# Routing of the last token tile in an attention, convolution and expert layer on one core: o-projection halves adjoined, weight splits moved to other places

## The chip, the cores and the metric

One core of a Trainium2 chip runs the whole layer in one launch. The metric is device time in microseconds, the median of several executions.

## What is computed

The kernel computes one layer for 1024 prompt tokens and 64 sample tokens (1088 rows of 1024 features). An attention branch and a gated short convolution are merged by sigmoid gates into m, and then come the parts that this document is about, all in float32 (shortened from the reference):

```
x = x + m @ w_o
h2 = rmsnorm(x, g_ffn)
g_logit = h2 @ w_rg + b_rg                  # 4 groups, the best one is taken
e_logit = (h2 @ w_re + b_re)[group]         # 8 experts in it, the best two are taken
gate = softmax(g_logit)[group] * top2(softmax(e_logit)) / sum(top2)
for each of 32 experts e, over the rows that chose it:
    y = (silu(h2 @ w1[e]) * (h2 @ w3[e])) @ w2[e]
x = x + sum over the two chosen experts of gate * y
x = x + sigmoid(rmsnorm(x, g_ple) @ w_pg) * (p @ w_ple)
```

The layer also returns the attention latents, the rotary keys and the convolution state.

## The kernel before, in words

The 1088 rows are nine tiles: tiles 0 to 7 of 128 rows and tile 8 of 64. A float32 product is made from three products of a rounded number type: each operand is split into a rounded part (`hi`, L56, a cast on ACT) and the rest (`lo`, L59, a subtraction, on VectorE unless another engine is named), and `mm3` (L61) multiplies hi by hi, hi by lo and lo by hi.

**The o-projection and the router.** `o_mm(i, b, fill)` makes half b (512 columns) of m @ w_o for tile i: 8 steps of k with three matmuls each. `fill` names functions to be called behind step k, which is how the steps of one tile's routing are put between another tile's matmuls on TensorE. `o_add` (L1051) adds a half to x on VectorE. `o_sq` squares a row on ACT and makes 1/rms on POOL (`rstd`, L84 and L85). `o_h2` (L1065) makes h2 on VectorE and stores h2 (`h2d`, L1067) and x (`x1d`, L1068) to DRAM from SP's queue. `o_tr` transposes four blocks of x (L1076) and splits them, `o_rt` multiplies them by the router's weights (L1087, L1089) and copies the result (lgT, L1093), `o_lg` transposes it back (L1098) and scales it into the logits lg (L1099, VectorE).

**Routing.** `route1(i)` is 20 short VectorE operations on the logits of tile i (L1123 to L1152): the group, the two experts, the one-hot matrices, and the running counts mc. `route2` makes each row's rank within its expert (L1158, L1159 on TensorE, L1161 to L1165 on VectorE; the two `am` operations are L1165). `route3` adds the tile to `tab` (L1172), the table of which row sits in which place of which expert. The tiles are routed in the order 0 to 5, 8, 6, 7. After the last tile the table becomes integer row numbers, `idx` (L1272).

**Experts.** `gather` (L1281) fetches up to 96 rows of h2d that an expert got, by an indirect DMA issued from POOL, into one of three buffers xg that were set to zero (L1341). `x_tr` transposes and splits the gathered rows (L1291, tiles xTh and xTl). Six weight blocks per expert, 128x1024 each, are loaded by SP into `eraw` (`e_load`, L894) and split by `e_hi` into weh on ACT and by `e_lo` into wel. SP takes its work in order, and a weight load also waits until the load five places ahead of it has landed (`w_dma`, DEEP = 5). There are 30 places for eraw, five experts' worth. The places of expert 3 are those of weights of the o-projection's first halves, and so come free when the last first half is done. `gate_values` (L1365 to L1376) turns logits into the gates, and `overflow_counts` (L1380 to L1409) counts rows beyond 96 per expert.

**What sets the order.** From the first `o_mm` up to `order.close()` the order on all five engines is that in which the code issues the work, written by hand. Behind `order.close()` a scheduler sets it. The code around the change:

```
    o_mm(7, 0, {5: [(route2, 5)]})
    o_add(7, 0)
    o_mm(8, 0, {0: [(route3, 5)]})
    ...
    e_load(4, (1, 4))
    o_tr(7, 1)
    o_h2(7)
    e_hi(0, 0)
    e_lo(0, 0, nc.gpsimd)
```

Of the kernel before, what the change touches and what calls it, by code (L numbers as in the profile page):

```python
# [7 lines left out]
F32 = mybir.dt.float32  # L8
# [3 lines left out]
AF = mybir.ActivationFunctionType  # L12
OP = mybir.AluOpType
# [7 lines left out]
D = 1024  # L21
# [4 lines left out]
EPS = 1e-6  # L26
# [8 lines left out]
A2 = 2 * T  # L35
DEEP = 5


@with_exitstack
def body(ctx, tc, a):  # L40
# [69 lines left out]
    def bank():  # L110
        return pb.tile([128, 512], F32, name="bk", tag="bk")
# [896 lines left out]
    gffn = xp2.tile([128, D], F32, name="gffn")  # L1008
    x1_, rs_, h2_, hb6, prt = {}, {}, {}, {}, {}

# [42 lines left out]
    def o_sq(i):  # L1053
        h2 = xp2.tile([128, D], F32, name="h2", bufs=1)
        ss = xp2.tile([128, 1], F32, name="ss4", bufs=2)
        n = TN[i]
        nc.scalar.activation(h2[:n], x1_[i][:n], AF.Square, accum_out=ss[:n])
        rs_[i] = xp2.tile([128, 1], F32, name="rs4", bufs=2)
        rstd(rs_[i][:n], ss[:n], 1.0 / D, 1)
        h2_[i] = h2  # L1060

    def o_h2(i):
# [46 lines left out]
    def small(name, *sh, dt=F32, bufs=2):  # L1109
        return xp2.tile([128] + list(sh), dt, name=name, bufs=bufs)  # L1110

    def g4(x):
        return x[:, :, None].to_broadcast([128, 4, 8])

    ed = edesc[:, None, :].to_broadcast([128, 4, 8])

    def route1(i):
        gl = lg[:, i, 0:4]
        el = lg[:, i, 4:36].rearrange("p (g e) -> p g e", g=4)
        d1, d2, oh1, oh2, es2 = (small(n, 4, 8, bufs=1) for n in ("d1", "d2", "oh1", "oh2", "es2"))  # L1120
        wg, wm = small("wg", 4), small("wm", 1)
        wm1, wm2 = small("wm1", 4), small("wm2", 4)
        V_.tensor_reduce(out=m1[:, i], in_=el, axis=AX.X, op=OP.max)  # L1123
        V_.tensor_reduce(out=gm[:, i:i + 1], in_=gl, axis=AX.X, op=OP.max)
# [7 lines left out]
        V_.scalar_tensor_tensor(out=es2, in0=oh1, scalar=-1e30, in1=el, op0=OP.mult, op1=OP.add)  # L1132
        V_.tensor_tensor(out=M[:, 0, i].rearrange("p (g e) -> p g e", g=4), in0=oh1, in1=g4(goh[:, i]), op=OP.mult)
        V_.tensor_reduce(out=m2[:, i], in_=es2, axis=AX.X, op=OP.max)
        V_.tensor_tensor(out=d2, in0=es2, in1=g4(m2[:, i]), op=OP.is_ge)
# [15 lines left out]
        else:  # L1151
            V_.tensor_tensor(out=mc, in0=MCs[r], in1=ms, op=OP.add)  # L1152
        MCs[r + 1] = mc

    def route2(i):
# [22 lines left out]
    for i in range(6):  # L1178
# [13 lines left out]
        if i >= 1:  # L1192
# [8 lines left out]
    e_load(1, (2, 5))  # L1201
    o_mm(7, 0, {5: [(route2, 5)]})
    o_add(7, 0)
    o_mm(8, 0, {0: [(route3, 5)]})
    o_add(8, 0)
    e_load(3)
    o_mm(8, 1, {6: [(o_tr, 8, 0)]})
    o_add(8, 1)
    o_sq(8)
    o_mm(6, 1, {1: [(o_tr, 8, 1), (o_h2, 8)], 3: [(o_rt, 8, 0, 8)],  # L1210
                5: [(o_lg, 8), (route1, 8)], 6: [(o_tr, 6, 0)]})
    o_add(6, 1)
    o_sq(6)
    e_load(4, (2, 5, 0, 3))
    o_mm(7, 1, {1: [(o_tr, 6, 1), (o_h2, 6)], 2: [(route2, 8)], 3: [(o_rt, 6, 0, 8)], 4: [(route3, 8)], 
                5: [(o_lg, 6), (route1, 6)], 6: [(o_tr, 7, 0)]})
    o_add(7, 1)
    o_sq(7)
    wbs.close()
# [37 lines left out]
    e_load(4, (1, 4))  # L1257
    o_tr(7, 1)
    o_h2(7)
    e_hi(0, 0)  # L1260
    e_lo(0, 0, nc.gpsimd)
    o_rt(7, 0, 8)
    route2(6)
    o_lg(7)
    route3(6)
    route1(7)
    for j in range(1, 6):
        e_hi(0, j)
    e_lo(0, 1, nc.gpsimd)
    route2(7)  # L1270
# [69 lines left out]
    for e in range(3):  # L1340
        nc.gpsimd.memset(xgs[e], 0.0)  # L1341
        gather(xgs[e][:CAP], idx[:CAP, 0, e:e + 1])
    for j in range(2, 6):
        e_lo(0, j)
    e_load(5)
    order.close()


    eps_, ep = opened("moe", bufs=2)
    x_tr(0, xgs[0], 0, ep, CAP)  # L1350
    x_tr(0, xgs[0], 1, ep, CAP)
    scr, pos = ep.tile([128, D], F32, name="y", bufs=NY), [0]
# [57 lines left out]

    gate_values()
    overflow_counts()

# [370 lines left out]
```

## Time and profile before

| | us |
|---|---|
| median of 3 runs | 1350.8 |
| the runs | 1348.19, 1350.80, 1350.96 |
| the profiled execution | 1351.81 |
| its span in the profile | 1349.8 |
| TensorE matmul busy | 1268.6 (94% of the span) |
| VectorE busy | 848.0 (63%) |
| ACT busy | 649.7 (48%) |
| POOL busy | 323.8 (24%) |

The shares are averages over the span. The profile's row of forty slices shows one place in the last half where TensorE is busy less than half of the time: the slice after 877 us has the digit 4 for TensorE and 6 for the granted clock. The chain of work that ended last is almost only TensorE's work at the program's end.

### The profile page before, as it was taken

How to read it: one execution, taken by the hardware profiler on the slowest of the kernel's cores; microseconds unless marked ns; L12 is line 12 of the kernel's file. 1: busy time of each engine (PE TensorE's matmuls, PEld its weight loads, DVE VectorE, ACT ScalarE, POOL GpSimd, SP SyncE). 2: the span in 40 equal slices, each digit the busy share in tenths (PEclk: the TensorE clock that was granted, in tenths of full speed). 3: DMA queues.
4: the chain of work that ended last, by engine and by line, in shares of the span. 5: the costliest groups of instructions: out<-in, count | busy, mean ns of one | idle time of the engine just before them, and what ended most of it. 6: DMA issues, size and time to landing. Idle time of an engine off the chain costs nothing. (4 is left out here: it accounts for less than half of the span.)

```text
span 1349.8 us, 20413 instructions
## 1 busy us (share of the span) xinstructions
PE 1268.6 (94%) x7235; PEld 1100.1 (81%) x7235; DVE 848.0 (63%) x1627; ACT 649.7 (48%) x1276; POOL 323.8 (24%) x375
## 2 busy tenths in 40 slices
PE   7999999998998999999999999749999999999998
PEld 6999999998987988888998888537666666667886
DVE  6433243325675466666659755678988889884743
ACT  6212142223344455555545211338888888886322
POOL 2000001124663333333315200232222222210210
PEclk9999999999998999999999999869999999999999
DMA  5111298734477523242257656769999999967511
GB/s 197 64 34 45 78 355 299 276 117 137 138 188 223 176 69 125 86 150 73 82 197 265 247 201 225 252 185 350 364 346 346 340 345 347 346 235 272 204 39 55
DMA packets 106057, 272.36 MB, mean 202 GB/s; under 512 B 13521, under 2 KB 42689, under 8 KB 105922
## 3 DMA queue, kind: packets, MB, share of 16 engines
q1 hardware_dynamic: 89968, 220.29, 47.1%
q0 software_dynamic: 15840, 50.68, 11.7%
q8 instruction: 58, 0.95, 0.3%
q14 instruction: 45, 0.37, 0.1%
q10 hardware_dynamic: 146, 0.07, 0.0%
HBM read 211.14 MB, written 67.19 MB: 206 GB/s over the span
## 5 line engine op out<-in xcount | busy, mean ns | idle before, releaser
L59 DVE TENSOR_TENSOR wel<-eraw,weh 128x1024 fp32r<-128x1024 f32 x190 | 226.3, 1220 | 34.4 <-ACT weh L56 32.4
L56 ACT CAST weh<-eraw 128x1024 fp32r<-128x1024 f32 x192 | 196.0, 1054 | 11.7 <-PE bk L64 10.7
L769 POOL TENSOR_TENSOR P<-P,ri 128x128 f32<-128x128 f32 (+8 forms) x72 | 77.2, 1077 | 129.2 <-DVE ri L768 109.6
L63 PE MATMUL bk<-wel,xTh 128*96 128x512 f32 x256 | 103.5, 404 | 1.5 <-DVE wel L59 1.4
L62 PE MATMUL bk<-weh,xTh 128*96 128x512 f32 x256 | 102.5, 400 | 1.7 <-ACT xTh L56 1.7
L64 PE MATMUL bk<-weh,xTl 128*96 128x512 f32 x256 | 103.1, 403 | 0.0
L1337 POOL DMA_INDIRECT Yd<-y,idx x32 | 41.3, 1292 | 227.2 <-ACT y L1334 217.5
L59 DVE TENSOR_TENSOR wl<-w_r,wh 128x1024 fp32r<-128x1024 f32 x28 | 34.3, 1225 | 75.7 <-ACT wh L56 75.3
L62 PE MATMUL bk<-hTAh,wh 128*128 128x384 f32 x224 | 76.6, 342 | 1.8 <-ACT hTAh L56 1.8
L63 PE MATMUL bk<-hTAl,wh 128*128 128x384 f32 x224 | 76.4, 341 | 0.0
L64 PE MATMUL bk<-hTAh,wl 128*128 128x384 f32 x224 | 76.1, 340 | 0.0
L62 PE MATMUL fg<-hTBh,fw 128*128 128x384 f32 (+1 forms) x224 | 74.9, 334 | 0.3 <-ACT fgm L605 0.2
L56 ACT CAST wh<-w_r 128x1024 fp32r<-128x1024 f32 x28 | 29.4, 1050 | 91.8 <-PE bk L63 86.3
L64 PE MATMUL fg<-hTBh,fw 128*128 128x384 f32 (+1 forms) x224 | 73.3, 327 | 0.0
L63 PE MATMUL fg<-hTBl,fw 128*128 128x384 f32 (+1 forms) x224 | 73.1, 326 | 0.0
L62 PE MATMUL bk<-hTBh,wh 128*128 128x384 f32 (+1 forms) x192 | 62.2, 324 | 0.0
L63 PE MATMUL bk<-hTBl,wh 128*128 128x384 f32 (+1 forms) x192 | 62.0, 323 | 0.0
L64 PE MATMUL bk<-hTBh,wl 128*128 128x384 f32 (+1 forms) x192 | 61.8, 323 | 0.0
L63 PEld LDWEIGHTS bk<-wel,xTh 128*96 128x96 f32 x256 | 41.7, 163 | 22.2 <-DVE wel L59 7.8
L62 PE MATMUL bk<-weh,ath 128*96 128x512 f32 x128 | 50.9, 397 | 8.8 <-ACT ath L56 8.8
L755 DVE TENSOR_REDUCE nm<-S 128x1 f32<-128x128 f32 (+8 forms) x72 | 50.8, 706 | 12.7 <-PE S L64 11.6
L62 PEld LDWEIGHTS bk<-weh,xTh 128*96 128x96 f32 x256 | 41.6, 162 | 19.3 <-ACT xTh L56 3.3
(782 smaller groups left out, 3750.8 us busy)
## 6 DMA issues: line engine op xcount, KB each, us to landing
eraw<-in_we_dram SPq DMA_DIRECT2D x192, 512.0 KB
fw<-wsd POOLq DMA_DIRECT2D x32, 512.0 KB, 4.3
w_r<-in_wing_dram SPq DMA_DIRECT2D x28, 512.0 KB
gm_r<-gscr SPq DMA_DIRECT2D x16, 544.0 KB
wsd<-wh SPq DMA_DIRECT2D x16, 512.0 KB
wsd<-wl SPq DMA_DIRECT2D x16, 512.0 KB
xy<-Yd SPq DMA_DIRECT2D x16, 512.0 KB
vd<-V SPq DMA_DIRECT2D x10, 512.0 KB
```

The source lines that it names most:

```text
L56: nc.scalar.copy(dst, src)
L59: (eng or nc.vector).tensor_tensor(out=dst, in0=src, in1=h.bitcast(F32), op=OP.subtract)
L62: r = nc.tensor.matmul(ps, sh, mh, start=first, stop=False)
L63: nc.tensor.matmul(ps, sh, ml, start=False, stop=False)
L64: nc.tensor.matmul(ps, sl, mh, start=False, stop=last)
L755: nc.vector.tensor_reduce(out=nm, in_=s, axis=AX.XY, op=OP.max, negate=True)
L769: nc.gpsimd.tensor_tensor(out=P[:, :nk], in0=P[:, :nk], in1=ri.to_broadcast([128, nk]), op=OP.mult)
L1337: nc.gpsimd.indirect_dma_start(out=Yd[:, :], out_offset=bass.IndirectOffsetOnAxis(ap=col, axis=0), in_=buf, in_offset=None, bounds_check=A ...
```

## The change

The o-projection halves of tile 7 are made last and next to each other. Before, the halves stood in the order (6,0), (7,0), (8,0), (8,1), (6,1), (7,1); now it is (6,0), (8,0), (8,1), (6,1), (7,0), (7,1). The steps of tile 6's routing, which stood behind (6,1) and partly behind (7,1), are put between the matmuls of (7,0) and (7,1); `route1` is cut in two for this. Tile 7's square is made by halves (`o_sq_half`), and its first transposes and first router matmuls stand within (7,1). POOL makes no weight splits any more: the six `lo` splits of expert 0 are VectorE's, two behind the gate values and four behind the transposition of the first gathered rows. Six `hi` casts stand behind the router instead of around it. Ten matmuls whose result nobody reads stand behind the last tab matmul (WARM). The weight loads of expert 3 are issued later. All line numbers rise by 1, by 15 behind `o_sq`, and by more further on.

```diff
...
+    def o_sq_half(i, b):
+        n = TN[i]
+        if b == 0:
+            h2_[i] = xp2.tile([128, D], F32, name="h2", bufs=1)
+            sqh[i] = xp2.tile([128, 2], F32, name="ss4h", bufs=1)
+        c = slice(512 * b, 512 * b + 512)
+        nc.scalar.activation(h2_[i][:n, c], x1_[i][:n, c], AF.Square, scale=1.0 / 32, accum_out=sqh[i][:n, b:b + 1])
+        if b == 1:
+            ss = sqh.pop(i)
+            rs = rs_[i] = xp2.tile([128, 1], F32, name="rs4", bufs=2)
+            nc.gpsimd.tensor_scalar(out=rs[:n], in0=ss[:n, 0:1], scalar1=ss[:n, 1:2], scalar2=EPS, op0=OP.add,
+                                    op1=OP.add)
+            nc.gpsimd.tensor_tensor(out=rs[:n], in0=rs[:n], in1=mhalf[:n, :1], op=OP.pow)
...
-    def route1(i):
+    def route1a(i):
...
+    def route1b(i):
+        d2, oh2, es2, wm2 = r1.pop(i)
         V_.tensor_reduce(out=m2[:, i], in_=es2, axis=AX.X, op=OP.max)
...
-    o_mm(7, 0, {5: [(route2, 5)]})
-    o_add(7, 0)
-    o_mm(8, 0, {0: [(route3, 5)]})
+    o_mm(8, 0, {5: [(route2, 5)]})
     o_add(8, 0)
-    e_load(3)
-    o_mm(8, 1, {6: [(o_tr, 8, 0)]})
+    o_mm(8, 1, {0: [(route3, 5)], 6: [(o_tr, 8, 0)]})
     o_add(8, 1)
     o_sq(8)
-    o_mm(6, 1, {1: [(o_tr, 8, 1), (o_h2, 8)], 3: [(o_rt, 8, 0, 8)],
-                5: [(o_lg, 8), (route1, 8)], 6: [(o_tr, 6, 0)]})
+    e_load(4, (2,))
+    o_mm(6, 1, {1: [(o_tr, 8, 1), (o_h2, 8)], 3: [(o_rt, 8, 0, 8)], 4: [(o_lg, 8), (route1, 8)],
+                6: [(o_tr, 6, 0)]})
     o_add(6, 1)
     o_sq(6)
-    e_load(4, (2, 5, 0, 3))
-    o_mm(7, 1, {1: [(o_tr, 6, 1), (o_h2, 6)], 2: [(route2, 8)], 3: [(o_rt, 6, 0, 8)], 4: [(route3, 8)], 
-                5: [(o_lg, 6), (route1, 6)], 6: [(o_tr, 7, 0)]})
+    e_load(4, (0, 3))
+    o_mm(7, 0, {0: [(o_tr, 6, 1)], 1: [(route2, 8), (o_h2, 6)], 2: [(o_rt, 6, 0, 8)], 3: [(route3, 8)],
+                4: [(o_lg, 6), (route1a, 6)]})
+    o_add(7, 0)
+    e_load(3)
+    e_load(4, (5,))
+    route1b(6)
+    o_mm(7, 1, {3: [(route2, 6), (o_tr, 7, 0), (o_sq_half, 7, 0)], 5: [(route3, 6)], 7: [(o_rt, 7, 0, 4)]})
     o_add(7, 1)
-    o_sq(7)
+    o_sq_half(7, 1)
+    o_tr(7, 1)
+    o_h2(7)
+    o_rt(7, 4, 8)
+    o_lg(7)
...
     e_load(4, (1, 4))
-    o_tr(7, 1)
-    o_h2(7)
-    e_hi(0, 0)
-    e_lo(0, 0, nc.gpsimd)
-    o_rt(7, 0, 8)
-    route2(6)
-    o_lg(7)
-    route3(6)
     route1(7)
-    for j in range(1, 6):
+    for j in range(6):
         e_hi(0, j)
-    e_lo(0, 1, nc.gpsimd)
     route2(7)
     route3(7)
...
-    for j in range(2, 6):
-        e_lo(0, j)
-    e_load(5)
-    order.close()
+    for _ in range(WARM):
+        nc.tensor.matmul(bank(), wsl[0, 0][0][:, 0:128], wsl[0, 0][0][:, 0:512], start=True, stop=True)
...
-    x_tr(0, xgs[0], 0, ep, CAP)
-    x_tr(0, xgs[0], 1, ep, CAP)
...
     gate_values()
+    e_lo(0, 0)
+    e_lo(0, 1)
+    x_tr(0, xgs[0], 0, ep, CAP)
+    x_tr(0, xgs[0], 1, ep, CAP)
+    for j in range(2, 6):
+        e_lo(0, j)
+    e_load(5)
+    order.close()
     overflow_counts()
```

On POOL, from 1/rms of tile 7 (rs) to the first gather, the kernel before has (rs of tile 6 ends in its first row)

```order
L85 TENSOR_TENSOR rs_9389<-rs_9389,mhalf 128x1
L84 TENSOR_SCALAR rs_9513<-ss_9511 128x1
L85 TENSOR_TENSOR rs_9513<-rs_9513,mhalf 128x1
L59 TENSOR_TENSOR wel<-eraw,weh 128x1024 x2
L1341 MEMSET xg_9635 128x1024
L1281 DMA xg_9635<-h2d,idx 96x1024
```

and the changed kernel

```order
L86 TENSOR_TENSOR rs_9353<-rs_9353,mhalf 128x1
L1073 TENSOR_SCALAR rs_9534<-ss4h 128x1
L1075 TENSOR_TENSOR rs_9534<-rs_9534,mhalf 128x1
L1364 MEMSET xg_9634 128x1024
L1304 DMA xg_9634<-h2d,idx 96x1024
```

The two weight splits are gone from between 1/rms and the zeroing of xg.

On VectorE, from the rank (rnk, am) and idx of the last tile on, the kernel before has these rows; y and gates are the gate values and, from L1382 on, the overflow counts:

```order
L1162 TENSOR_REDUCE rnk<-pr 128x2
L1165 TENSOR_SCALAR am<-c_7557,rnk 128x96 x2
L1272 TENSOR_SCALAR idx<-tab 96x64
L59 TENSOR_TENSOR wel<-eraw,weh 128x1024 x4
L1365 TENSOR_TENSOR y<-lg,gm 128x36
L1372 TENSOR_REDUCE y<-m_7553 128x9
L1397 MEMSET y 1x24
L1368 TENSOR_REDUCE y<-y 128x9
L1374 SCALAR_TENSOR_TENSOR y<-y 128x9
L1375 RECIPROCAL gates<-y 128x9
L1376 TENSOR_TENSOR gates<-gates,y 128x9
L59 TENSOR_TENSOR xTl_9671<-bk,xTh_9670 128x384
```

In the changed kernel, from the end of the gate values on (idx stands six rows ahead of the first row shown):

```order
L1390 TENSOR_REDUCE y<-m_7553 128x9
L1392 SCALAR_TENSOR_TENSOR y<-y 128x9
L1393 RECIPROCAL gates<-y 128x9
L1394 TENSOR_TENSOR gates<-gates,y 128x9
L60 TENSOR_TENSOR wel<-eraw,weh 128x1024 x2
L1400 TENSOR_SCALAR y<-bk 128x32
L60 TENSOR_TENSOR xTl_9686<-bk,xTh_9685 128x384
L1402 CAST y<-y 128x32
L60 TENSOR_TENSOR xTl_9695<-bk,xTh_9694 128x384
L60 TENSOR_TENSOR wel<-eraw,weh 128x1024 x4
L1403 TENSOR_SCALAR y<-y 128x32
```

The four splits that followed idx at once now follow the gate values (two, in place of POOL's) and the two xTl of the first expert (four), and the overflow operations come later.

On SP, from the load of x for tile 8 to the last stores of h2 and x (tile 7), the kernel before issues

```order
L1013 DMA x_9179<-in_x_dram 64x1024
L894 DMA eraw<-in_we_dram 128x1024 x8
L1067 DMA h2d<-h_9281 64x1024
L1068 DMA x1d<-x_9179 64x1024
L894 DMA eraw<-in_we_dram 128x1024 x4
L1067 DMA h2d<-h_9386 128x1024
L1068 DMA x1d<-x_9029 128x1024
L894 DMA eraw<-in_we_dram 128x1024 x2
L1067 DMA h2d<-h_9510 128x1024
L1068 DMA x1d<-x_9031 128x1024
L894 DMA eraw<-in_we_dram 128x1024 x162
```

and the changed kernel

```order
L1014 DMA x_9179<-in_x_dram 64x1024
L895 DMA eraw<-in_we_dram 128x1024 x3
L1082 DMA h2d<-h_9243 64x1024
L1083 DMA x1d<-x_9179 64x1024
L895 DMA eraw<-in_we_dram 128x1024 x2
L1082 DMA h2d<-h_9350 128x1024
L1083 DMA x1d<-x_9029 128x1024
L895 DMA eraw<-in_we_dram 128x1024 x7
L1082 DMA h2d<-h_9506 128x1024
L1083 DMA x1d<-x_9031 128x1024
L895 DMA eraw<-in_we_dram 128x1024 x164
```

Seven weight loads stand ahead of the last h2d store, where there were two; the five are missing ahead of the store of tile 8 (the 64-row one).

## Rows read from the trace of the kernel before

**Rows 1.** Windows: length, busy us of PE, PEld, DVE, ACT, POOL, clock, DMA share, GB/s.

```profile
870.00:880.00 10.00, 4.59 (x27) 3.88 (x28) 8.14 (x16) 7.56 (x10) 7.04 (x5) 0.51 0.59 216
880.00:890.00 10.00, 0.73 (x3) 0.41 (x2) 8.87 (x32) 0.33 (x2) 5.06 (x2) 0.50 0.43 134
890.00:900.00 10.00, 3.41 (x14) 2.66 (x15) 1.92 (x8) 0.96 (x2) 4.44 (x5) 0.50 0.73 217
900.00:910.00 10.00, 9.69 (x47) 6.63 (x46) 9.60 (x19) 7.72 (x10) 0.96 (x1) 0.95 0.59 175
910.00:920.00 10.00, 10.00 (x51) 7.20 (x50) 9.64 (x14) 9.14 (x14) 2.47 (x2) 1.00 0.99 329
...
960.00:1100.00 140.00, 135.73 (x670) 95.46 (x669) 123.11 (x144) 116.93 (x174) 34.48 (x28) 1.00 0.99 346
```

**Rows 2.** Timeline of TensorE: start, length, line, operation, count, idle before and releaser.

```profile
859.60 0.65 PE L1076 MATMUL bk<-ident,x 128*128 128x128 f32 x4 [1.38 <-DVE x L1051]
...
864.98 0.31 PE L1098 MATMUL bk<-id,lgT 72*128 72x36 f32 x2
...
866.56 0.39 PE L63 MATMUL bk<-wo71l,mT 128*128 128x512 f32 x1
866.79 0.40 PE L64 MATMUL bk<-wo71h,mT 128*128 128x512 f32 x1
870.10 1.01 PE L1076 MATMUL bk<-ident,x 128*128 128x128 f32 x4 [2.91 <-DVE x L1051]
...
873.93 0.64 PE L1098 MATMUL bk<-id,lgT 72*128 72x36 f32 x2 [0.33 <-ACT lgT L1093]
...
896.59 1.51 PE L1291 MATMUL bk<-ident,xg 96*128 96x96 f32 x8 [12.79 <-DMA xg<-h2d,idx]
...
899.85 0.63 PE L63 MATMUL bk<-wel,xTh 128*96 128x512 f32 x1
```

**Rows 3.** Timeline of VectorE, 863 to 898 us.

```profile
863.59 0.45 DVE L1165 TENSOR_SCALAR am<-c,rnk 128x96 fp32r<-128x96 f32 x2
...
874.16 4.98 DVE L1165 TENSOR_SCALAR am<-c,rnk 128x96 fp32r<-128x96 f32 x2
878.17 0.97 DVE L1099 SCALAR_TENSOR_TENSOR lg<-bk,rs,brt 128x36 f32<-128x36 f32 x1
...
883.83 0.22 DVE L1272 TENSOR_SCALAR idx<-tab 96x64 int32<-96x64 f32 x1 [0.46 <-PE tab L1172]
883.97 4.62 DVE L59 TENSOR_TENSOR wel<-eraw,weh 128x1024 fp32r<-128x1024 f32 x4
...
898.01 0.56 DVE L59 TENSOR_TENSOR xTl<-bk,xTh 128x384 fp32r<-128x384 f32 x1 [8.03 <-ACT xTh L56]
```

**Rows 4.** Timeline of POOL, 872 to 968 us.

```profile
872.77 5.41 POOL L59 TENSOR_TENSOR wel<-eraw,weh 128x1024 fp32r<-128x1024 f32 x2 [0.59 <-ACT weh L56]
...
884.92 4.65 POOL L1281 DMA_INDIRECT xg<-h2d,idx  x1 [5.85 <-issue]
...
890.83 1.00 POOL L1281 DMA_INDIRECT xg<-h2d,idx  x1 [0.28 <-POOL xg L1341]
...
967.31 1.15 POOL L1281 DMA_INDIRECT xg<-h2d,idx  x1 [0.30 <-PE bk L1317]
```

**Rows 5.** Timeline of VectorE under the gather at 967.31.

```profile
966.39 3.50 DVE L59 TENSOR_TENSOR wel<-eraw,weh 128x1024 fp32r<-128x1024 f32 x3 [0.20 <-ACT weh L56]
```

**Rows 6.** DMA queues from 880 to 892 us: packets, MB, share of 16 engines.

```profile
q1 hardware_dynamic: 526, 1.92, 50.2%
```

**Rows 7.** Timeline of SP's DMA issues, 832 to 874 us.

```profile
832.59 0.43 SPq L1068 DMA_DIRECT2D x1d<-x  x1
836.24 0.49 SPq L1013 DMA_DIRECT2D x<-in_x_dram  x1
...
873.69 0.33 SPq L1067 DMA_DIRECT2D h2d<-h  x1
```

**Rows 8.** Page, costliest groups: busy, mean ns, idle before and its releaser.

```profile
L59 DVE TENSOR_TENSOR wel<-eraw,weh 128x1024 fp32r<-128x1024 f32 x190 | 226.3, 1220 | 34.4 <-ACT weh L56 32.4
```

More of the change, by code (lines that the diff above doesn't have):

```diff
@@ L36 @@
 DEEP = 5
+WARM = 10
 @with_exitstack
@@ L1008, in body @@
     gffn = xp2.tile([128, D], F32, name="gffn")
-    x1_, rs_, h2_, hb6, prt = {}, {}, {}, {}, {}
+    x1_, rs_, h2_, hb6, prt, sqh = {}, {}, {}, {}, {}, {}
     def o_load(i):
@@ L1115, in body @@
     ed = edesc[:, None, :].to_broadcast([128, 4, 8])
-    def route1(i):
+    r1 = {}
+    def route1a(i):
         gl = lg[:, i, 0:4]
@@ L1122, in route1 @@
         wm1, wm2 = small("wm1", 4), small("wm2", 4)
+        r1[i] = d2, oh2, es2, wm2
         V_.tensor_reduce(out=m1[:, i], in_=el, axis=AX.X, op=OP.max)
@@ L1153, in route1 @@
         MCs[r + 1] = mc
+    def route1(i):
+        route1a(i)
+        route1b(i)
     def route2(i):
```

## The prediction

> **What bounds the kernel now.** I read three views in turn. First the windows, for the engines by stretch [rows 1]. From 960 to 1100 us, in the loop over the experts, TensorE is busy 135.73 of 140 us and VectorE 123.11: the loop is TensorE's, VectorE is close behind, and the DMA share is 0.99. Only 3 per cent is free there, so time that the loop gets at its start or loses there is kept to the end. Between 870 and 900 it is different: TensorE is busy 4.59, 0.73 and 3.41 of 10 us, at a granted clock of 0.50 to 0.51, the lower of its two levels (1.2 of 2.4 GHz). That is the hole which the change works on: the routing of the last tile, then the first gather.
>
> Then TensorE's timeline through the hole [rows 2]. The last o-projection matmul starts at 866.79 and ends 0.40 later. The transposes of tile 7 begin at 870.10, after 2.91 us of waiting for VectorE's sum; the transposes of the first gathered rows begin at 896.59, after 12.79 us of waiting for the gather to land. So the hole is one chain: sum, transposes, router, logits, routing on VectorE, idx, gather, landing. Whatever shortens it moves the expert loop forward.
>
> Last, VectorE and POOL in that stretch [rows 3, 4]. The pair of am operations, 0.45 us for tile 8, takes 4.98 us at 874.16, while POOL runs its two lo splits from 872.77 to 878.18; the logits of tile 7 stand behind that pair and start at 878.17, though their matmuls ended at 873.93 + 0.64 = 874.57. idx ends at 883.83 + 0.22 = 884.05. POOL starts the first gather at 884.92 and is at it for 4.65 us; the second takes 1.00. It landed at 896.59, 7.02 after the 889.57 at which POOL was done.
>
> **Part one: idx comes earlier.** Terms, all on the chain:
> - The sum of tile 7 no longer stands behind tile 6's whole routing, which is now split and interleaved. TensorE has nothing to do for 2.91 us in the kernel before; what has to remain is about the 0.7 us of one half's addition and its hand-over. I take 2.2 off, and put 0.3 back, since routing steps of tile 5 now stand in front of shorter runs of matmuls and may wait: -1.9. Bounds: 0 (the sum is as late as before) to -2.3.
> - With so short a wait I expect the clock to stay up. A wait of 1.38 us at 859.60 left it up: these four transposes took 0.65, those of tile 7 after 2.91 us of waiting took 1.01, and the two logit matmuls 0.31 against 0.64 [rows 2]. That is 0.36 + 0.33, and 0.1 for the square done by halves: -0.8 (bounds 0 to -1.2, if the router's last matmuls halve as well).
> - With no split on POOL, the am pair of tile 6 takes its 0.45 and is done inside the last matmuls. The logits start behind their own matmul: they end some 0.3 after it, where they ended at 878.17 + 0.97 = 879.14, or 4.57 after it: -4.3. This is the surest term.
> - Two gate operations of 0.1 us each leave the routing of tile 7: -0.2.
>
> Sum: 7.2 us; idx ends near 876.8. The Trainium skill ("SBUF — State Buffer", section "Who interferes with whom") says that a tensor_scalar in its two-port form and GpSimd lock each other out for a whole instruction. The row of 4.98 us for the am pair agrees.
>
> **Part two: the first gather.** The change puts VectorE's four splits (4.62 us from 883.97) behind the gather's issue. Is it they that made it 4.65 us? For it: they ended at 888.59, and the gather at 889.57, which is 0.98 later, the length of an undisturbed gather [rows 3, 4]. Against it: the gather at 967.31 ran under three splits back to back (966.39, 3.50 us) and took 1.15 [rows 4, 5], as the others of the loop did. And it is the first gather of the program: something paid once would look the same. No instruction queue moved anything from 880 to 892, only q1 did [rows 6]; that speaks against code being fetched then, but not against other first-time work. I hold the once-paid cost for likelier: 4.65 stays, and with it the start 0.87 after idx. Bounds of this term: 0 to -(4.65 - 0.96) - (0.87 - 0.29) = -4.3, the second from POOL's usual 0.28 between two steps.
>
> Two rules of the Trainium skill pull the same way. "GPSIMD Engine Reference", section "Instruction dispatch", says that the first call of a freshly loaded kernel pays about 6 us once; by that page the gather would stay long and the sum would keep its 7.2. "SBUF — State Buffer" (same section as above) says that a tensor_tensor has no two-port form and takes only the read side of the shared ports, while making descriptors needs the write side; by that the splits never held the gather up, which speaks against what this change would gain there. The 1.15 us at 967.31 agrees with it; the 0.98 above does not.
>
> **Part three: what is given back.** Two splits that POOL made are now VectorE's, but lie in its wait for the landing (nothing else was there: its next work after the gate values began at 898.01). The four others now stand behind the transposed lo halves of the first expert, so behind the landing. There VectorE is busy 9.60 and 9.64 of 10 us [rows 1], so 4.62 us of extra work find 0.40 + 0.36 us free; the rest delays the splits of the second expert, and TensorE with them: +3.9. Bounds: 0 (the overflow operations, which move back behind splits, make room) to +4.62. I take 3.9 since both engines are nearly full there.
>
> **Part four: costs that I put at nothing.** Ten filler matmuls follow the last tab matmul: at most 0.63 each as at the low clock [rows 2], 6.3 us, in TensorE's own 12.79 us of waiting. Their cover goes only if the gather lands within 6.3 us of idx, and its transfer alone took 7.02. Would they keep the clock up? They end some 5 us or more before the landing, and 2.91 us without work were enough for 1.01 us transposes; so nothing is gained. If it were, the first expert's six matmuls of 0.63 would be shorter, by less than 1.5 us. Six ACT casts move behind the lgT copy: ACT is free there.
>
> On SP, seven weight loads are put ahead of the two stores of tile 7, where there were two. Their buffers are free when the first half of tile 7 is done, one half (24 matmuls at 0.23) before the last matmul's end: 867.2 - 5.6 = 861.6. At the loop's 346 GB/s [rows 1] a 512 KB load takes 1.5 us, seven 10.6: the last lands near 872.2, about when h2 of tile 7 is ready. A store took 3.65 us, from 832.59 to the load at 836.24 that waited for it [rows 7]. So h2d lands near 875.9, a little ahead of idx at 876.8, and the gather waits for idx. In the kernel before, it was issued at 873.69, 10.4 ahead of idx's end: that reserve is spent.
>
> **Sum.** 7.2 - 3.9 = 3.3 us. The profiled execution took 1351.81 us (its span 1349.8), which is 1.0 over the median of 1350.8. 1351.8 - 3.3 = 1348.5, at the median 1347.5.
>
> **Rivals.**
> - *The splits held the gather up.* For it the 0.98, against it the 1.15 at 967.31. Then the term of part two is -4.3: 3.3 + 4.3 = 7.6 us, so 1343.2 at the median.
> - *The store is late (the slower side).* Everything up to idx is as above, but the seven loads take the rate of 870 to 880, 216 GB/s: 7 x 2.4 = 17 us, to 878.6, and 3.65 for the store: 882.2, 5.4 after idx. The gather waits for it: 3.3 - 5.4 = -2.1, so 1352.9. It decides from a landing at 876.8 on, and eats the whole gain at 880.1. Against it: that window's rate holds idle queues, since its DMA share is 0.59; for it: nothing is left of the reserve, and buffers may come free late.
> - *The loop takes it all.* If the weight stream (share 0.99) or VectorE paces the loop and not its start, an earlier landing moves nothing: 1350.8. Against it: of VectorE's 34.4 us of waiting for splits, 32.4 were for ACT's casts, so 2.0 at most for loads [rows 8]. It would also be the outcome if the splits' delay were more than its bound.
>
> **How the numbers follow.** The forecast case, gather as long as before: 0.5. Splits held it up: 0.3. Nothing gained: 0.12. Store late: 0.08. The likeliest gives 1347.5. Its own range, with the idx term 6 to 8 and the given-back 2 to 4.62: 1344.8 to 1349.4. The whole range reaches down into the second case, 1342.0 (its 1343.2 with part of the backlog hidden), and up over the third, 1351.0; outside are the late store and the ends. A measurement of this kernel tells about 0.2% (2.7 us), so faster means under 1348.1: nearly all of the second case (0.29) and 0.6 of the first (0.30), some 0.59. Slower: 0.08 of the late store and 0.01. The same: 0.32.
>
> **What the profile after would show.** The am pair of tile 6 at 0.45 and the logits of tile 7 at 0.26; idx ended near 876.8; no split on POOL. The first gather's own row decides part two: 4 us or more, or near 1. Its start should be under 1 us after idx; 2 us or more with idx done means the store. Transposes of the gathered rows near 889.4 (forecast) or 885 (rival). Then waits of TensorE for wel and xTl in the first two experts, some 4 us more than before: if they are missing, part three is wrong; and if the fillers keep the clock at 1.00 to the first expert, part four.

## The result and the profile after

The changed kernel takes 1341.15 us (median; 1337.65 to 1342.22) against 1350.2 us of the kernel before on the same chip: ratio 0.9927, interval 0.9912 to 0.9942. A second measurement of it gave 0.9925 (0.9912 to 0.9939). By the two ratios that is 9.9 and 10.1 us; the median of 1341.15 against the 1350.8 that the forecast started from gives 9.7. Forecast were 3.3 us, and the time lies below the range given (1342.0 to 1351.0).

The profiled executions took 1351.81 and 1341.73 us (spans 1349.8 and 1339.8). Part of that difference lies ahead of the change: the first store of h2, ahead of which the texts of the two programs do the same, starts at 763.89 us in the one and at 761.25 in the other (SP's DMA issues, before and after; the last two rows are used below):

```profile
763.89 0.33 SPq L1067 DMA_DIRECT2D h2d<-h  x1
```

```profile
761.25 0.33 SPq L1082 DMA_DIRECT2D h2d<-h  x1
...
857.02 7.33 SPq L895 DMA_DIRECT2D eraw<-in_we_dram  x7
869.13 0.33 SPq L1082 DMA_DIRECT2D h2d<-h  x1
```

This start moved between 759.4 and 763.9 us over all the profiles of this study, with no change in what is done ahead of it. So the times below are counted from that store. From there to the end before takes 585.9 us and after 578.6: 7.4 us less.

The windows of the changed kernel (columns as in [rows 1]):

```profile
870.00:880.00 10.00, 5.18 (x16) 3.74 (x16) 7.42 (x34) 5.03 (x7) 4.42 (x5) 0.66 0.81 259
880.00:890.00 10.00, 8.28 (x39) 5.53 (x38) 8.76 (x14) 4.07 (x6) 4.68 (x4) 0.83 1.00 270
890.00:900.00 10.00, 8.47 (x43) 5.86 (x42) 8.71 (x12) 8.49 (x13) 0.00 (x0) 1.00 1.02 363
```

From 870 to 900 us TensorE is now busy 5.18, 8.28 and 8.47 of 10 us, where it was busy 4.59, 0.73 and 3.41 [rows 1]. The ten fillers are 4.41 us of the added 13.2; the other 8.8 are work that lay further back before. TensorE's timeline (columns as in [rows 2]) shows its ends:

```profile
865.88 0.66 PE L1091 MATMUL bk<-ident,x 128*128 128x128 f32 x4 [0.28 <-DVE x L1052]
...
868.96 0.41 PE L1113 MATMUL bk<-id,lgT 72*128 72x36 f32 x2 [0.41 <-ACT lgT L1108]
...
874.11 4.41 PE L1367 MATMUL bk<-weh 128*128 128x512 f32 x10
879.78 0.85 PE L1314 MATMUL bk<-ident,xg 96*128 96x96 f32 x8 [1.25 <-DMA xg<-h2d,idx]
...
887.08 0.52 PE L1314 MATMUL bk<-ident,xg 96*128 96x96 f32 x4 [1.46 <-DMA xg<-h2d,idx]
```

The last transposes of tile 7 wait 0.28 us (2.91 before) and take 0.66 (1.01); the gathered rows are transposed at 879.78. VectorE and POOL:

```profile
862.19 0.45 DVE L1190 TENSOR_SCALAR am<-c,rnk 128x96 fp32r<-128x96 f32 x2
...
869.41 0.26 DVE L1114 SCALAR_TENSOR_TENSOR lg<-bk,rs,brt 128x36 f32<-128x36 f32 x1 [0.34 <-PE bk L1183]
...
874.34 0.22 DVE L1295 TENSOR_SCALAR idx<-tab 96x64 int32<-96x64 f32 x1 [0.46 <-PE tab L1197]
...
876.59 2.35 DVE L60 TENSOR_TENSOR wel<-eraw,weh 128x1024 fp32r<-128x1024 f32 x2
...
881.92 4.62 DVE L60 TENSOR_TENSOR wel<-eraw,weh 128x1024 fp32r<-128x1024 f32 x4
```

```profile
875.43 1.13 POOL L1304 DMA_INDIRECT xg<-h2d,idx  x1 [5.30 <-DMA eraw<-in_we_dram]
...
877.81 2.01 POOL L1304 DMA_INDIRECT xg<-h2d,idx  x1 [0.27 <-POOL xg L1364]
...
882.33 1.63 POOL L1304 DMA_INDIRECT xg<-h2d,idx  x1 [0.30 <-issue]
```

The am pair of tile 6 takes 0.45 (4.98 before, [rows 3]), the logits of tile 7 0.26 (0.97), and idx ends at 874.56. The first gather starts 0.87 us later, as before, but takes 1.13 us in place of 4.65 [rows 4], and lands at 879.78, which is 3.22 us after POOL was done with it, in place of 7.02.

Counted from the first store:

| | before | after | difference |
|---|---|---|---|
| idx ends | 120.16 | 113.31 | -6.85 |
| gather starts | 121.03 | 114.18 | -6.85 |
| POOL is done with it | 125.68 | 115.31 | -10.37 |
| gathered rows are there | 132.70 | 118.53 | -14.17 |
| 22nd copy of an expert's result | 248.71 | 238.59 | -10.12 |
| end of the span | 585.91 | 578.55 | -7.36 |

The copies of the experts' results on ACT, of which the 22nd stands in the table, tell how far the loop has come (before, then after):

```profile
1012.60 0.58 ACT L1334 COPY y<-bk 96x512 f32<-96x512 f32 x1
```

```profile
999.84 0.58 ACT L1357 COPY y<-bk 96x512 f32<-96x512 f32 x1
```

So 14.2 us were won up to the landing; 4.1 were given back at the start of the loop and 2.8 more from the 22nd copy to the end. From the third copy to the 52nd the difference stays at 10.1 us, so the start's loss lies ahead of the first copies and the end's behind the 52nd. In the second profile of the changed kernel the three amounts were 14.1, 5.7 and 1.3.

### The profile page after: what moved, and what is told of

Same layout as the page of the kernel before. It is cut to its first block, busy times and chain, and to the rows that moved or that the text cites. A ratio compares the mean times of both kernels' runs of the same rounds, so it can differ in the third digit from the quotient of the medians.

```text
span 1339.8 us, 20433 instructions
## 1 busy us (share of the span) xinstructions
PE 1272.8 (95%) x7245; PEld 1102.1 (82%) x7245; DVE 842.7 (63%) x1629; ACT 650.1 (49%) x1278; POOL 317.9 (24%) x373
```

## The experiments

All ratios are to the kernel before, timed in between on the same chip. The last three columns are profile times against before's, counted from the first store, as in the table above. One profile places the end within some 2.5 us of what the ratio says, so for the end the ratio decides.

| kernel | ratio (interval) | median us | landing | 22nd copy | end |
|---|---|---|---|---|---|
| after, first measurement | 0.9927 (0.9912 to 0.9942) | 1341.15 | -14.2 | -10.1 | -7.4 |
| after_rep | 0.9925 (0.9912 to 0.9939) | 1340.35 | -14.1 | -8.4 | -7.1 |
| b_splits | 1.0003 (0.9989 to 1.0016) | 1350.33 | -11.6 | -3.7 | -0.3 |
| b_splits_fill | 0.9951 (0.9936 to 0.9965) | 1343.39 | -11.5 | -8.0 | -6.5 |
| a_oldsplits | 1.0009 (0.9999 to 1.0020) | 1351.63 | -3.4 | +2.4 | +3.1 |
| a_early4 | 0.9975 (0.9963 to 0.9988) | 1346.23 | -6.1 | -4.3 | -3.0 |
| a_dummyTT | 0.9990 (0.9976 to 1.0004) | 1348.83 | -10.2 | -2.6 | +0.3 |
| a_dummyRed | one time, 1344.31 | | -14.1 | -9.2 | -6.2 |
| a_nofill | 0.9970 (0.9957 to 0.9983) | 1346.16 | -13.9 | -6.1 | -3.3 |
| a_hand10 | 0.9973 (0.9960 to 0.9985) | 1346.60 | -13.8 | -5.6 | -2.8 |
| a_hand0 | 0.9948 (0.9936 to 0.9960) | 1343.31 | -14.2 | -6.2 | -4.5 |
| a_ms10 | 0.9929 (0.9916 to 0.9942) | 1340.47 | -13.0 | -10.3 | -10.0 |
| a_ms3_10 | 0.9923 (0.9906 to 0.9939) | 1340.36 | -13.0 | -9.0 | -9.7 |

The theory that the experiments put to the test, theory 1, is that the splits on VectorE held the first gather up, in its issue and, by freeing places for weight loads, in its landing. Its rivals are that the new order of the routing took the gather's length away, and that the gather does not matter.

### Do the splits hold the gather up?

**a_early4** puts four of the splits straight behind idx again:

```diff
     V_.tensor_scalar(out=idx[...], in0=tab[:CAP], scalar1=NOROW, scalar2=None, op0=OP.add)
+    for j in range(4):
+        e_lo(0, j)
...
     gate_values()
-    e_lo(0, 0)
-    e_lo(0, 1)
     x_tr(0, xgs[0], 0, ep, CAP)
     x_tr(0, xgs[0], 1, ep, CAP)
-    for j in range(2, 6):
+    for j in range(4, 6):
         e_lo(0, j)
```

> The changed kernel with four of its six VectorE splits straight behind idx, ahead of the gate values, and two behind the transposes of the first gathered rows. Theory 1: gather row 4 us or more (it ends about 1 us behind the last of the four), landing about 7 us behind it, so the first transposes some 7 us later than in the changed kernel; the backlog behind the landing is 2.3 us smaller: 3 to 5 us slower than the changed kernel. Rival (splits do not matter to the gather): row near 1.1, landing 3.2 behind it, and 0 to 2 us faster than the changed kernel, since less is left behind the landing.

Its first gather on POOL, and TensorE's first transposes of gathered rows:

```profile
876.01 4.66 POOL L1306 DMA_INDIRECT xg<-h2d,idx  x1 [5.30 <-DMA eraw<-in_we_dram]
```

```profile
888.45 1.51 PE L1316 MATMUL bk<-ident,xg 96*128 96x96 f32 x8 [9.42 <-DMA xg<-h2d,idx]
```

The gather is back at 4.66 us, done at 880.67, and lands at 888.45, 7.8 us later. Against the second measurement of the changed kernel it loses 0.9975 - 0.9925 = 0.5% (6.7 us), more than the 3 to 5 expected, though the two intervals leave room for 5.

**a_dummyTT** leaves the splits where the change has them and adds four subtractions of the same shape, whose results are written again later:

```diff
     V_.tensor_scalar(out=idx[...], in0=tab[:CAP], scalar1=NOROW, scalar2=None, op0=OP.add)
+    for j in range(4):
+        lo(wsl[0, j][1], wsl[0, j][2], wsl[0, j][0])
```

> The changed kernel plus four extra subtractions on VectorE straight behind idx, of the same shape as the splits and writing the same lo tiles that the real splits write again later; they free no place for a weight load. They tell the two halves of theory 1 apart. If two-input VectorE work holds up the issue: gather row 4 us or more, but landing still about 3.2 us behind it. If it is the freed weight loads alone that made it late: gather row near 1.1. In either case 2.5 to 5 us slower than the changed kernel, since the two real splits now end 4.6 us later, behind the old landing.

VectorE, POOL and TensorE of it:

```profile
875.67 4.62 DVE L60 TENSOR_TENSOR wel<-eraw,weh 128x1024 fp32r<-128x1024 f32 x4
```

```profile
876.63 4.66 POOL L1306 DMA_INDIRECT xg<-h2d,idx  x1 [5.87 <-DMA eraw<-in_we_dram]
```

```profile
884.48 1.51 PE L1316 MATMUL bk<-ident,xg 96*128 96x96 f32 x8 [4.97 <-DMA xg<-h2d,idx]
```

Again 4.66 us; the four subtractions end at 880.29, the gather at 881.29. But it lands at 884.48, 3.2 us later. Its total is 0.65% (8.8 us) above the changed kernel's, more than the 2.5 to 5 expected, and doesn't price the gather alone: the second expert's transposes came to stand behind one matmul there, and behind them TensorE waits 1.02 us for wel and 0.86 for xTl. The two kernels differ in what the queue of the weight loads (q1) carried from 876 to 890 us (packets, MB, share of 16 engines; first a_early4, then a_dummyTT):

```profile
q1 hardware_dynamic: 630, 2.25, 50.1%
```

```profile
q1 hardware_dynamic: 53, 0.15, 2.6%
```

In a_early4 the real splits set places of eraw free, and 2.25 MB of weight loads moved beside the gathers; in a_dummyTT 0.15 MB did. Over all fourteen profiles the landing is 6.84 to 7.78 us behind POOL's end in the three kernels with real splits straight behind idx (before, a_oldsplits, a_early4), and 3.11 to 3.44 in the others. So the splits cost the gather two things: 3.5 us of POOL's time, by being on VectorE, and some 4 us of its transfer, by releasing loads.

**a_dummyRed** has four sums in the same place, which read one input each:

```diff
+    dred = xp2.tile([128, 4], F32, name="dred", bufs=1)
     V_.tensor_scalar(out=idx[...], in0=tab[:CAP], scalar1=NOROW, scalar2=None, op0=OP.add)
+    for j in range(4):
+        V_.tensor_reduce(out=dred[:, j:j + 1], in_=wsl[0, j][2], axis=AX.X, op=OP.add)
```

> The changed kernel plus four extra sums over 1024 elements on VectorE straight behind idx, each with one input in SBUF and hardly any output, where a_dummyTT had four subtractions with two inputs. If the second input is what holds the gather up: its row near 1.1 us though VectorE is busy throughout. If any VectorE work does: 4 us or more.

```profile
876.10 4.58 DVE L1298 TENSOR_REDUCE dred<-eraw 128x1 f32<-128x1024 f32 x4
```

```profile
877.05 1.13 POOL L1307 DMA_INDIRECT xg<-h2d,idx  x1 [5.53 <-DMA eraw<-in_we_dram]
```

VectorE is busy for 4.58 us and the gather takes 1.13. So VectorE's being busy does not hold POOL up; something that the subtraction has and the sum lacks does. That is the second input or the full-size output (128x1024 against 128x1), and this pair does not tell which. The Trainium skill ("SBUF — State Buffer", section "Who interferes with whom") has a rule that names the input: a VectorE instruction with two inputs in SBUF contends with a GpSimd instruction that reads SBUF, and the gather reads idx there. 4.66 against 1.13 agrees with it. The sentence of the same section that the prediction leaned on, that a tensor_tensor takes only the read side while making descriptors needs the write side, did not foretell this gather's 4.66.

### What each half of the change is worth

**b_splits** is the kernel before with the split places of the change, no fillers:

```diff
-    e_lo(0, 0, nc.gpsimd)
...
-    e_lo(0, 1, nc.gpsimd)
...
     gate_values()
+    e_lo(0, 0)
+    e_lo(0, 1)
+    x_tr(0, xgs[0], 0, ep, CAP)
+    x_tr(0, xgs[0], 1, ep, CAP)
+    for j in range(2, 6):
+        e_lo(0, j)
+    e_load(5)
+    order.close()
     overflow_counts()
```

> The kernel before, with its own order of o-projection halves and routing, but with the six lo splits of expert 0 on VectorE where the change puts them (two behind the gate values, four behind the transposes of the first gathered rows); no split on POOL, no filler matmuls. Theory 1 (the splits held the first gather up, in its issue and, by freeing places for weight loads, in its landing): am pair of tile 6 at 0.45 us, idx about 4.4 us earlier, the first gather's row near 1.1 us and its landing some 3.2 us behind that, so about 11.7 us earlier at the landing, of which 5 to 6 are given back: 5 to 7 us faster than before. Rival (the gather was long for a reason that the new routing order took away): gather row still above 4 us, landing 7 us behind it, 1 to 2 us faster than before.

The first landing came 11.6 us earlier, as theory 1 had it, and the time did not move at all (1.0003). Both expectations of the time were wrong. TensorE shows why:

```profile
880.52 1.51 PE L1289 MATMUL bk<-ident,xg 96*128 96x96 f32 x8 [5.45 <-DMA xg<-h2d,idx]
...
887.01 1.51 PE L1289 MATMUL bk<-ident,xg 96*128 96x96 f32 x8 [3.88 <-DMA xg<-h2d,idx]
...
901.25 0.33 PE L1315 MATMUL bk<-ident,sa 96*128 96x96 f32 x2
```

Behind two matmuls of the first expert stand the transposes of the second expert's rows, for which TensorE waits 3.88 us; they and the matmuls that follow run slowly (the transposes take 1.51 us, in the changed kernel 0.85). This place is the scheduler's, behind `order.close()`. In the changed kernel these transposes stand behind 12 matmuls. The difference is the ten fillers: they lengthen TensorE's part ahead of the loop. The last row, the transposes of the first expert's second stage (sa), is used further down.

**b_splits_fill** is b_splits with the change's ten filler matmuls, and nothing else:

```diff
+    for _ in range(10):
+        nc.tensor.matmul(bank(), wsl[0, 0][0][:, 0:128], wsl[0, 0][0][:, 0:512], start=True, stop=True)
     eps_, ep = opened("moe", bufs=2)
```

> The kernel b_splits (before's order of routing, the change's split places) with the ten filler matmuls added, with which the scheduler puts the second expert's transposes behind 14 to 15 matmuls of the first. Theory (splits moved away from the gather are worth several us, and b_splits lost them to the early placing of these transposes): landing as in b_splits, 11 to 12 us earlier than before, no wait of 3.9 us at the second expert's transposes, 3 to 6 us faster than before. Rival (without the new routing order the earlier landing is swallowed by the loop): within 1 us of before.

```profile
881.96 0.85 PE L1289 MATMUL bk<-ident,xg 96*128 96x96 f32 x8 [1.06 <-DMA xg<-h2d,idx]
...
889.01 0.85 PE L1289 MATMUL bk<-ident,xg 96*128 96x96 f32 x8 [2.60 <-DMA xg<-h2d,idx]
...
897.81 0.33 PE L1315 MATMUL bk<-ident,sa 96*128 96x96 f32 x2
```

The transposes now stand behind 13 matmuls and wait 2.60 us, the landing is the same, and the kernel is 0.49% (6.6 us) faster than before. So the splits' places and the fillers together, without the new order of the routing, give two thirds of the whole. The remaining third, 0.26% (3.5 us, with intervals that leave 1 to 6), comes with the new order.

**a_nofill** is the changed kernel without its fillers:

```diff
-WARM = 10
+WARM = 0
```

> The changed kernel without its ten filler matmuls (WARM = 0). Theory (the fillers work through the scheduler: without them it puts the transposes of the second expert's rows after three matmuls of the first expert, where TensorE then stands until the second gather lands): a wait of about 4 us at those transposes, the low clock until about 10 us later, 4 to 6 us slower than the changed kernel. Rival (they do nothing but keep the clock up, or nothing): 0 to 1.5 us slower.

```profile
879.11 1.51 PE L1314 MATMUL bk<-ident,xg 96*128 96x96 f32 x8 [5.50 <-DMA xg<-h2d,idx]
...
885.98 1.51 PE L1314 MATMUL bk<-ident,xg 96*128 96x96 f32 x8 [4.22 <-DMA xg<-h2d,idx]
```

As expected: the second transposes, behind two matmuls, wait 4.22 us. Its ratio of 0.9970 makes it 0.45% (6.1 us) slower than the changed kernel. The granted clock (length, TensorE busy, clock, DMA share, GB/s) was at its lower level (1.2 GHz) to 890 us:

```profile
886.00:890.00 4.00, 4.00 (x15) 0.50 1.00 353
```

**a_hand10** and **a_hand0** take the order away from the scheduler. The first expert's matmuls and the second one's transposes are written by hand, with ten fillers and with none:

```diff
     x_tr(0, xgs[0], 1, ep, CAP)
-    for j in range(2, 6):
-        e_lo(0, j)
+    w13_mm(0, 0, 4, CAP)
+    e_lo(0, 2)
+    e_lo(0, 3)
+    w13_mm(0, 4, 6, CAP)
+    x_tr(1, xgs[1], 0, ep, CAP)
+    w13_mm(0, 6, 8, CAP)
+    x_tr(1, xgs[1], 1, ep, CAP)
+    e_lo(0, 4)
+    e_lo(0, 5)
     e_load(5)
...
```

(Behind the "..." the loop leaves out the steps that are now written ahead of it.)

> The changed kernel with the first expert's matmuls and the transposes of the second expert's rows in an order written by hand: 18 matmuls, four transposes, 6 matmuls, four transposes, with the ten fillers. If the waiting for the second gather and the scheduler's placing are what the first microseconds lose: its wait of 1.46 us is gone and the loop runs 0 to 2 us ahead of the changed kernel's. If VectorE's splits pace this stretch anyway: the same time within 1 us.

> The same hand-written order without fillers. Beside a_hand10 it shows what the fillers are worth when they cannot move the order: if it is the clock, the first transposes take 1.5 us in place of 0.85 and some ten matmuls more run at the low clock, 1 to 2.5 us slower than a_hand10; if nothing, the same.

Both expectations missed. a_hand10 is slower than the changed kernel by 0.48% (6.5 us), though its wait for the second gather is gone: the scheduler now put the first expert's second stage early, and TensorE waits 2.72 us for VectorE there (a_hand10, then a_hand0):

```profile
879.47 0.85 PE L1314 MATMUL bk<-ident,xg 96*128 96x96 f32 x8 [1.31 <-DMA xg<-h2d,idx]
...
892.00 0.55 PE L1340 MATMUL bk<-ident,sa 96*128 96x96 f32 x2 [2.72 <-DVE sa L1333]
```

```profile
881.15 1.51 PE L1314 MATMUL bk<-ident,xg 96*128 96x96 f32 x8 [5.53 <-DMA xg<-h2d,idx]
...
893.52 0.35 PE L1340 MATMUL bk<-ident,sa 96*128 96x96 f32 x2 [2.72 <-DVE sa L1333]
```

And with fillers it is slower than without: 0.9973 against 0.9948. The first transposes are faster with them (0.85 against 1.51 us), but behind these both kernels run seven matmuls at the lower clock, both wait 2.72 us for sa, and at the 22nd copy nothing is left of the difference (-5.6 and -6.2). Why the two then end 3.3 us apart in their medians is open; their orders on VectorE differ in a few rows too. So the pair shows only that faster first transposes are worth nothing in this order. What a clock that stays up would be worth in the scheduler's order it does not show. In the changed kernel itself the clock (columns as above) was

```profile
878.00:880.00 2.00, 0.75 (x5) 0.96 0.76 197
...
882.00:884.00 2.00, 2.00 (x6) 0.50 0.91 258
884.00:886.00 2.00, 1.63 (x5) 0.76 1.04 238
```

The ten fillers bring it to its upper level (2.4 GHz) as they end, and then it is back at the lower one from 882 on, while TensorE is busy with the first expert; from 885 it stays up. That is about as far behind the landing as before, where the matmul at 899.85 still took 0.63 [rows 2]. The clock does not always fall there: in the second profile of the changed kernel it was at its lower level from 888 to 890, and b_splits_fill held the upper one where b_splits had the lower (b_splits, then b_splits_fill):

```profile
886.00:892.00 6.00, 4.99 (x17) 0.50 1.02 313
```

```profile
886.00:892.00 6.00, 3.40 (x20) 1.00 0.99 251
```

From the first gathered transposes to the transposes of sa, b_splits takes 20.73 us (880.52 to 901.25) and b_splits_fill 15.85 (881.96 to 897.81). Of these 4.88 us TensorE's listed waits give 1.06; the rest is, in the main, the same matmuls at the higher clock. The same stretch is 4.33 us shorter in the changed kernel than in a_nofill, and there waits give 2.49. So the fillers' gain comes with both a later place of the second expert's transposes and a higher clock, and no run here separates the two.

**a_oldsplits** is the other half: the change's order of halves and routing with the old places of the splits, no fillers.

```diff
-    o_tr(7, 1)
-    o_h2(7)
-    o_rt(7, 4, 8)
-    o_lg(7)
...
     e_load(4, (1, 4))
+    o_tr(7, 1)
+    o_h2(7)
+    e_hi(0, 0)
+    e_lo(0, 0, nc.gpsimd)
+    o_rt(7, 4, 8)
+    o_lg(7)
     route1(7)
-    for j in range(6):
+    for j in range(1, 6):
         e_hi(0, j)
+    e_lo(0, 1, nc.gpsimd)
...
-    for _ in range(WARM):
-        nc.tensor.matmul(bank(), wsl[0, 0][0][:, 0:128], wsl[0, 0][0][:, 0:512], start=True, stop=True)
+    for j in range(2, 6):
+        e_lo(0, j)
+    e_load(5)
...
     gate_values()
-    e_lo(0, 0)
-    e_lo(0, 1)
...
-    for j in range(2, 6):
-        e_lo(0, j)
-    e_load(5)
```

> The changed kernel's order of halves and routing, but with the splits of expert 0 where the kernel before has them (two on POOL, four on VectorE straight behind idx) and without the filler matmuls. Theory 1: the first gather's row is again 4 us or more, its landing about 7 us behind, so that only the earlier idx is left: 2 to 4 us faster than before. Rival (the order took the gather's length away): gather row near 1.1 us, landing 3 to 4 us behind, 6 to 9 us faster than before.

(Two more weight loads come ahead of the last store of h2 this way. It was still issued 107.85 us behind the first store, and 107.88 in the changed kernel.)

The gather is long, as theory 1 had it, but the kernel is not faster at all (1.0009). POOL and, under its splits, two short operations of tile 7's routing on VectorE:

```profile
868.09 5.41 POOL L60 TENSOR_TENSOR wel<-eraw,weh 128x1024 fp32r<-128x1024 f32 x2 [0.55 <-ACT weh L57]
...
879.02 4.66 POOL L1307 DMA_INDIRECT xg<-h2d,idx  x1 [4.63 <-DVE idx L1298]
```

```profile
869.84 1.40 DVE L1143 TENSOR_TENSOR d<-lg,m 128x32 f32<-128x32 f32 x1
871.17 2.36 DVE L1144 SCALAR_TENSOR_TENSOR wg<-lg,gm,c 128x4 f32<-128x4 f32 x1
```

POOL's two splits now fall on the routing of tile 7 in place of the am pair of tile 6, and two operations of 0.19 and 0.22 us take 1.40 and 2.36. The earlier routing is worth 3.4 us at the landing while POOL splits, and the loop then loses 5.8 us up to the 22nd copy; what makes that more than the 4.1 of the changed kernel was not tried.

### Could it be better?

**a_ms10** sets all three buffers to zero ahead of the first gather, so that the gathers follow one another; **a_ms3_10** also puts a third split ahead of the landing.

```diff
     for e in range(3):
         nc.gpsimd.memset(xgs[e], 0.0)
+    for e in range(3):
         gather(xgs[e][:CAP], idx[:CAP, 0, e:e + 1])
...
     e_lo(0, 1)
+    e_lo(0, 2)
     x_tr(0, xgs[0], 0, ep, CAP)
     x_tr(0, xgs[0], 1, ep, CAP)
-    for j in range(2, 6):
+    for j in range(3, 6):
         e_lo(0, j)
```

The lines behind the "..." are a_ms3_10's alone.

> The changed kernel with the three buffers of gathered rows set to zero ahead of the first gather, so that POOL issues the first three gathers one behind the other. If TensorE's wait for the second gather (1.5 to 3.2 us) is what the first expert loses: the second gather is issued 1 to 1.5 us earlier and lands as much earlier, 1 to 2.5 us faster than the changed kernel. If the transfers share one rate and only the order of issue moves: the same time.

> a_ms10 with a third of expert 0's lo splits ahead of the landing, where VectorE waits 1.75 us in the changed kernel, and three behind it. If the backlog behind the landing costs what it measures: 0.5 to 1.2 us faster than a_ms10. If the scheduler's placing of the second expert's transposes (here behind some 20 matmuls) is worth more than the backlog: 1 to 3 us faster than the changed kernel even if a_ms10 is not.

POOL and TensorE of a_ms10:

```profile
874.98 1.90 POOL L1364 MEMSET xg<- 128x1024 f32 x2 [3.75 <-DMA x1d<-x]
```

```profile
887.90 0.82 PE L1314 MATMUL bk<-ident,xg 96*128 96x96 f32 x8
```

The second gather's wait is gone (its transposes at 887.90 have none), but the two memsets on POOL now run beside the last tile's am pair, which takes 1.24 us in place of 0.45, so that idx ends 1.0 us later and the first gather lands 1.2 us later than in the changed kernel:

```profile
874.75 1.24 DVE L1190 TENSOR_SCALAR am<-c,rnk 128x96 fp32r<-128x96 f32 x2
```

The one seems to make up for the other: the ratios are 0.9929 and 0.9923 against 0.9925, no difference that these measurements can tell.

**after_rep** is the changed kernel once more:

> The changed kernel itself once more, in more rounds, since the stretch ahead of the first h2d store differs by up to 4.5 us from one profile to the next without any change in it. From the first h2d store to the end the changed kernel's profile was 7.4 us shorter than before's, so if the rest was chance the ratio is near 0.9945; if the change also moved the part ahead of it, near 0.9927.

It came out at 0.9925, where the expectation put a gain ahead of the first store too, though its profile was again only 7.1 us shorter from that store on. The starts of that store do not bear such a gain out: the two other kernels with before's order of routing, b_splits and b_splits_fill, reach it at 759.37 and 760.78 us, the changed kernel and its variants between 760.27 and 762.75. The one profile of before reached it latest of all, at 763.89, so its part ahead of the store may be long by chance and the part behind it short. What the other 2.5 us of the measured gain are stays open.

## Why the prediction was wrong

**Part one held.** idx was to come 7.2 us earlier; it came 6.85. The am pair went to 0.45 us, the logits to 0.26 right behind their matmuls, the transposes of tile 7 to 0.66 after a wait of 0.28. Its four terms, counted from the end of the last o-projection matmul, measured -2.1 (forecast -1.9), -1.0 (-0.8), -4.3 (-4.3) and 0.0 (-0.2), and the o-projection itself ended 0.55 us later.

**Part two failed, and this is the step that made the forecast wrong.** I held it "for likelier" that the 4.65 us of the first gather were paid once. The first gather of the changed kernel took 1.13, against 0.96 to 1.00 of later undisturbed ones, so at most 0.17 us are paid once; four subtractions bring 4.66 back and four sums don't. The rival had it right, and its term, -4.3, nearly so: the row lost 3.52, the start 0.87 after idx stayed. My evidence against it was the gather at 967.31 under three splits, at 1.15 us [rows 4, 5]. It was misread. Three splits in 3.50 us end each 1.17 us; the first of them ended near 967.56, and the gather 0.90 after that, at 968.46. The one at 882.33 in the changed kernel ended at 883.96, 0.88 after the first split's end (881.92 + 4.62 / 4 = 883.08), and the one at 877.81 ended at 879.82, 0.88 after the splits did. So by their ends these gathers were held up as well, to the next end of a split, where the first gather of the kernel before waited for the last of four. Being the first is not the reason. A later gather of a_ms3_10 took 4.58 us under four splits and ended 0.85 after the last of them, while one in a_nofill was through 0.86 after the third (POOL and VectorE of a_ms3_10, then POOL and VectorE of a_nofill):

```profile
917.13 4.58 POOL L1304 DMA_INDIRECT xg<-h2d,idx  x1 [0.30 <-issue]
```

```profile
916.24 4.62 DVE L60 TENSOR_TENSOR wel<-eraw,weh 128x1024 fp32r<-128x1024 f32 x4
```

```profile
918.83 2.00 POOL L1304 DMA_INDIRECT xg<-h2d,idx  x1 [0.30 <-issue]
```

```profile
916.48 4.65 DVE L60 TENSOR_TENSOR wel<-eraw,weh 128x1024 fp32r<-128x1024 f32 x4
```

What decides whether a gather gets through between two splits is open.

**A term was missing.** I took the 7.02 us from POOL's end to the landing for fixed. It was 3.22, since the splits that were moved no longer release weight loads just then: 3.80 us, as much as the row itself. The list of what a moved step issues has to go one step further, to the transfers that wait for its inputs to be free.

**Part three, what is given back,** was put at 3.9; it measured 4.1 and 5.7 at the 22nd copy, and 2.8 and 1.3 more from there to the end, where the scheduler's order differs; that end was not tried by itself. Its cause was only partly the one I gave. VectorE is indeed full there (8.76 and 8.71 of 10 us), but TensorE also waits there 1.46 to 3.17 us for the second gather, of which I said nothing.

**Part four failed for the fillers.** I gave them nothing, since the clock would not keep over 5 us or more up to the landing. The landing came so much earlier that they ended only 1.26 us ahead of it (878.52 and 879.78). They are worth 6.1 us in the changed kernel and 6.6 in b_splits_fill, by the order that the scheduler then makes and by the clock, which kept in b_splits_fill and fell for some matmuls in the changed kernel; the runs do not separate the two. The order is what the forecast had no term for. That was to be seen in the order of the program: with the fillers the second expert's transposes stand behind 12 matmuls, without them behind two.

The store of h2 was not late: it was issued at 869.13 behind the seven loads, 5.4 us ahead of idx's end, and the first gather started 0.87 us after idx as before.

**The sum.** Forecast: 7.2 - 3.9 = 3.3. The profile: 6.85 + 3.52 + 3.80 - 4.05 - 2.76 = 7.36. The splits' rival, at 7.6, was right about the gather; that it comes so near to 7.36 is luck, since it lacked the landing's 3.8 and gave back 3.9 in place of 6.8. The measured 1341.15 lies below the range's 1342.0: that end held neither the landing's 3.8 nor the 2.5 us that the profiles don't place.

## What to carry to other kernels

Before a two-input VectorE pass is left beside an indirect gather on the critical path, look at the gather's row in the same kernel with nothing beside it, and compare ends, not lengths: a gather that ends a fixed time after a VectorE instruction (here 0.83 to 1.00 us) may have waited for it. Ask of each moved instruction which buffers it releases, and which transfers start then. And where a scheduler orders what follows a hand-written part, read its new order for each variant: an instruction that looks like padding can be worth something by the place that it gives others.

## What the runs showed of the hardware

- The first gather issued from POOL took 1.11 to 1.13 us alone and under four single-input sums, and 4.65 or 4.66 in all four kernels that had four two-input subtractions back to back behind idx. A later one took 4.58 in a_ms3_10.
- The first gather landed 3.11 to 3.44 us behind POOL's end in the eleven profiles without real splits straight behind idx, and 6.84 to 7.78 in the three with them.
- Splits on POOL stretch short VectorE operations on tiny tiles as well: 0.19 and 0.22 us became 1.40 and 2.36, and the pair of 0.45 became 4.98 [rows 3]. A memset on POOL made that pair 1.24.
- In the changed kernel the granted clock rose from 0.50 to 0.96 as 4.4 us of filler matmuls ended, and was 0.50 again 3 us later, between 882 and 884 us, with TensorE busy in that window throughout. In b_splits_fill, with the same fillers, it was 1.00 from 886 to 892.
